# First stage of a two-layer pooling-and-attention block: pooling bands built on the chip, x loaded first, a new written order, and 32 transposes ahead of it

## The chip, the cores and the metric

The kernel runs on one core of a Trainium2 chip. The metric is device time in microseconds (us) from start to end of one execution. Before the change three runs took 1154.93, 1154.96 and 1155.19 us; the median is 1154.96 us. The core's engines each work through a queue of their own, in order: TensorE (PE in the profile, its weight loads PEld), VectorE (DVE), ScalarE (ACT), GpSimd (POOL) and SyncE (SP), which here issues the DMA transfers.

## The reference

The program computes two layers over 512 latent tokens and 256 context tokens of width 1024, in float32. Layer 0 mixes tokens by centred mean pooling, layer 1 by attention; each is followed by a squared-ReLU MLP with 4096 hidden units. The part that the change touches is the beginning of layer 0:

```python
def rms_norm(x, g):
    y = x * lax.rsqrt(jnp.mean(x * x, axis=-1, keepdims=True) + EPS)
    return y * g
...
m = (jax.nn.silu(cond) @ w + b)              # adaLN: shift, scale, gate for both halves of a layer
h_lat = modulate(rms_norm(x, g_mix_pre[i]), sh1, sc1)
y_lat = pool_mixer(h_lat, w_pool[j], pool_scale[j])
x = x + gt1 * rms_norm(y_lat, g_mix_post[i])
m_lat = sq_relu_mlp(modulate(rms_norm(x, g_mlp_pre[i]), sh2, sc2), w_mlp_in[i], w_mlp_out[i])
...
# pool_mixer: group g (256 channels) has window w = 2, 4, 8, 16
diff = mean over [t - w/2, t + w/2) of hf, minus hf
outs.append(diff @ w_pool[g])
```

The context tokens go through the same with their own conditioning vector. In layer 0 each of six modulation vectors (SH1, SC1, GT1, SH2, SC2, GT2) is a product of silu(cond) with a 1024 x 1024 block of `w_ada`.

## The kernel before

Tokens lie on the 128 partitions in six tiles t: 0 to 3 are latent, 4 and 5 context. `xr` holds the residual stream and `acc` what is being worked on. Products that need float32 accuracy are split in a high and a low part (hi and lo), and three products are summed.

The **first stage** is everything up to the first MLP group. Its steps stand in a table of words, `FIRST`, which is walked in order; while it is walked, the instructions of TensorE, VectorE and ScalarE are kept in the order in which they are recorded (`Kept`, lines 78 to 89). GpSimd and SyncE are not bound by it. The words, with the tile or channel block after the colon (a star puts a step on ScalarE rather than VectorE):

- `xs` sums the squares of a tile of x (ScalarE), `xe` adds epsilon (VectorE), `xp` takes the power -1/2 (GpSimd), `xn` scales the tile by it into `acc`.
- `edge` copies the inner band matrix and puts in the columns for the two ends of a sequence; `psm` and `psc` multiply a tile with its band on TensorE, which gives pooled mean minus identity, transposed (latent into `psm`, context into `psc`); `ev`, `evc` copy those results out of PSUM.
- `mm` is a conditioning product: one or two loads of 1 MB from `w_ada` (named `raw` in SBUF), multiplied on TensorE into `psada`; `rows`, `sel` and `mods` turn the result into columns. `SC1_0` to `SH1_3` come in eight loads, `GT1` in four, `SC2` and `SH2` in eight, twenty in all.
- `hi`, `lo` scale the pooled columns, `pool` multiplies them by `w_pool` (into `pspool`). Then, per tile: `ms` sums squares of the result, `rs` makes the reciprocal root, `c` copies, `b` multiplies by the gate, `r` adds to the residual, `s` and `rs2` are the next norm, `n` scales.
- `turn` transposes (into `psx`), `h` modulates, `xhi` and `xlo` split, `whi` and `wlo` split the first MLP weights, and `in` multiplies with them (into `psin`): this is the first group of the MLP, and the last thing in the table.

`rs` and `rs2` call a helper, `rstd`, that issues two GpSimd instructions, a TENSOR_SCALAR that adds epsilon (`ms` in the profile, lines 208 and 214) and the power (`rs`, line 216).

The inner bands (four windows, 128 x 144 each) and the edge columns come ready from the host in one transfer, `gate<-in_band`, of 128 x 640 numbers. SyncE issues the transfers in the order of the code: a small one with the conditioning vectors (`phase`), tiles 0 and 1 of x, the bands, tiles 2 to 5, `vec`, the pooling weights, then the `w_ada` loads. The buffers for `raw` come from two pools of four and three, by a list `turns`.

After the table, the first MLP goes on group by group on TensorE (lines 637, 761, 884), with VectorE and ScalarE preparing the weights and, for the following layers, the remaining modulation vectors on VectorE.

An activation function table is loaded into ScalarE when a function is not in the one that is loaded. To have the table of Exp at hand for the attention, `extra0` issues one Exp on a constant in group 2 of the first MLP (line 1108); the instruction depends on nothing else, and in the program it stands first in ScalarE's queue.

Of the kernel before, what the change touches and what calls it, by code (L numbers as in the profile page):

```python
# [17 lines left out]
P = 128  # L18
D = 1024
KT = D // P  # L20
# [21 lines left out]
xs:0 xe:0 xp:0 xn:0 xs:1 xe:1 xs:2 edge:0 xp:1 psm:0:2 xn:1 xs:3 psm:0:0 xe:2 psm:0:4 xp:2 psm:1:2 xs:4 xn:2  # L42
psm:1:4 psm:0:6 xe:3 xp:3 edge:1* psm:2:4 xe:4 psm:2:2 xp:4 xn:3 xs:5 psm:1:0 psm:3:4 psm:3:2 ev:4* xe:5 psm:2:0
xp:5 xn:4* psm:3:0 pw:0 ev:5* psm:1:6 wsc:0 psm:2:6 psm:3:6 pw:1 ev:7* ev:6 wph:0 wsc:1 mm:SC1_0 ev:0* psc:4:0
rows:SC1_0 xn:5 mm:SH1_0 wph:1 sel:SC1_0 ev:2* rows:SH1_0 psc:5:0 mods:SC1_0 psc:4:2 evc:0 sel:SH1_0 psc:5:2
mods:SH1_0 mm:SC1_1 wpl:0 hi:0 psc:4:6 rows:SC1_1 evc:2* psc:5:6 lo:0 hi:1 mm:SH1_1 sel:SC1_1 evc:6* psc:4:4
mods:SC1_1 psc:5:4 rows:SH1_1 lo:1 sel:SH1_1 evc:4* mm:SC1_2 mods:SH1_1 pool:0:0 rows:SC1_2 hi:2 wpl:1 pool:5:0
hi:3 sel:SC1_2 mm:SH1_2 lo:2 pool:1:0 mods:SC1_2 rows:SH1_2 sel:SH1_2 mm:SC1_3 mods:SH1_2 lo:3 hi:4 pool:4:0
pool:1:1 lo:4 mm:SH1_3 ms:1:0 rows:SC1_3 hi:5 pool:4:1 rows:SH1_3 c:1:0 sel:SC1_3 sel:SH1_3 pool:5:1 mods:SH1_3
mods:SC1_3 pool:0:1 lo:5 hi:7 mm:GT1_0a hi:6 lo:7 pool:0:2 mm:GT1_0b ms:4:0 lo:6 pool:5:2 rows:GT1_0 pool:0:3  # L50
c:4:0 sel:GT1_0 ms:0 mm:GT1_2a mods:GT1_0 gc:1:0 gc:0:0 psg:0:0 rs:0 c:0 pool:1:2 gate:0:0 mm:GT1_2b w_in
psg:1:0 rows:GT1_2 pool:1:3 gate:1:0 b:1:0 sel:GT1_2 pool:2:0 whi:0 mods:GT1_2 gc:0:1 gc:1:1 b:4:0 psg:0:1
ms:1:1 pool:5:3 wlo:0 gate:0:1 pool:4:2 rs:1 c:1:1* b:0 pool:4:3 ms:5 psg:1:1 b:1:1 pool:2:1 ms:4:1 rs:5 r:0
mm:SC2_0a c:4:1* gate:1:1 rs:4 mm:SC2_0b r:1 c:5* pool:2:2 s:0 b:4:1 pool:3:0 r:4 s:1 pool:3:1 rs2:0 pool:3:2
rows:SC2_0 s:4 rs2:1 pool:2:3 b:5 n:0* mm:SH2_0a rs2:4 n:1 mm:SH2_0b ms:2 r:5 sel:SC2_0 n:4* turn:0:1 rows:SH2_0
# [37 lines left out]

@with_exitstack
def backbone(ctx: ExitStack, tc, x, ctx_in, w_ada, w_pool, w_qkv, g_q, g_k, w_o, w_mlp_in,
             w_mlp_out, vecs, rope, band, out):
    nc = tc.nc
    ordered, mixed = [False], [False]
    sy, gp = nc.sync, nc.gpsimd
# [1506 lines left out]
```

## Time and profile before

| what | value |
|---|---|
| median of three runs | 1154.96 us |
| the profiled execution's own time | 1155.58 us |
| its span from first to last instruction | 1153.7 us |
| TensorE busy | 1135.3 us (98%) |
| VectorE busy | 930.9 us (81%) |
| ScalarE busy | 632.1 us (55%) |
| GpSimd busy | 71.1 us (6%) |
| TensorE's first matmul starts | 8.29 us |
| first matmul after the table (line 637) starts | 92.39 us |
| granted TensorE clock | 0.999 |

In a line of the timeline the first number is the start in us from the beginning of the span, the second the duration; then come engine, line, operation, output and input, the number of instructions taken together, and in brackets how long the engine had been idle and what released it. Nearly every instruction of the first stage has line 91, that of the helper that records it, so tiles and names tell the steps apart. The granted clock is a figure of the throttle; the rate at which TensorE takes its instructions is read from the starts of the matmuls.

### The profile page before, as it was taken

To read this page: it belongs to the slowest core of one execution; us is meant where nothing else is said; L and a number is where in the kernel's file an instruction comes from. 1 tells how busy PE (TensorE), PEld (TensorE's weight loads), DVE (VectorE), ACT (ScalarE), POOL (GpSimd) and SP (SyncE) were. 2 spreads that over 40 slices of the span, in tenths; PEclk is the share of its full clock that TensorE was granted. 3 is DMA by queue.
4 is the path that set the end of the run, shared out by engine and by line. 5 is a ranking of instruction groups with operands and counts; after the bars stand their busy time and mean duration, and the time that the engine had idled before them with its cause. 6 is when DMAs were issued, how large, how long until landed. Compare 5 with 4: busy or idle time off the path is not lost.

```text
span 1153.7 us, 16000 instructions
## 1 busy us (share of the span) xinstructions
PE 1135.3 (98%) x6200; PEld 988.7 (86%) x6200; DVE 930.9 (81%) x1517; ACT 632.1 (55%) x1082; POOL 71.1 (6%) x113
## 2 busy tenths in 40 slices
PE   7999999999999999999999999999999999999997
PEld 6779899988899988998887889988988888888886
DVE  4788588998988997996778699867787679778876
ACT  7687445554455444455675367753776435534523
POOL 1230000000000000000241200002100000000001
PEclk9999999999999999999999999999999999999999
DMA  9982233333343444333422102115243214313312
GB/s 376 419 350 75 74 116 113 137 120 141 113 150 140 146 147 146 120 137 115 177 74 73 37 1 74 38 74 186 106 159 133 91 56 146 110 45 138 110 33 114
DMA packets 25516, 147.34 MB, mean 128 GB/s; under 512 B 2784, under 2 KB 5344, under 8 KB 9696
## 3 DMA queue, kind: packets, MB, share of 16 engines
q1 hardware_dynamic: 25440, 146.32, 35.0%
q8 instruction: 49, 0.80, 0.3%
q14 instruction: 27, 0.22, 0.1%
HBM read 138.96 MB, written 7.34 MB: 127 GB/s over the span
## 4 chain that ended last, share of the span: by engine, by line
PE 90%; issue 3%; POOL 3%; DVE 2%; ACT 2%; DMA 0%; POOLq 0%; DVEq 0%; SPq 0%; ACTq 0%
PE pso L884 24%; PE psin L761 18%; PE psin L637 16%; PE pso L995 12%; PE psy L1421 3%; PE po L1396 3%; PE pss L1355 3%; PE psq L1141 2%; PE pspt L1377 2%; PE psin L91 2%; PE psada L91 1%; POOL rs L216 1%; PE psm L91 1%; PE pspool L91 1%; POOL rs L1150 1%
## 5 line engine op out<-in xcount | busy, mean ns | idle before, releaser
L884 PE MATMUL pso<-units,rb 128*128 128x512 f32 x1152 | 279.2, 392 | 0.0
L884 PEld LDWEIGHTS pso<-units,rb 128*128 128x128 f32 x1152 | 214.7, 188 | 41.0
L303 DVE SCALAR_TENSOR_TENSOR rows<-raw,cond,rows 128x256 f32<-128x256 f32 x280 | 127.0, 478 | 2.0
L898 DVE TENSOR_TENSOR acc<-acc,pso 128x512 f32<-128x512 f32 x126 | 83.9, 679 | 39.5 <-PE pso L884 39.4
L637 PE MATMUL psin<-ra,rb 128*128 128x512 f32 (+1 forms) x310 | 87.8, 360 | 0.0
L995 PE MATMUL pso<-units,pairs 128*128 128x512 f32 x336 | 82.7, 389 | 0.0
L637 PE MATMUL psin<-ra 128*128 128x512 f32 (+1 forms) x256 | 76.5, 376 | 0.0
L995 PEld LDWEIGHTS pso<-units,pairs 128*128 128x128 f32 x336 | 63.1, 188 | 13.1
L999 DVE TENSOR_TENSOR acc<-acc,pso 128x512 f32<-128x512 f32 x72 | 48.7, 682 | 26.3 <-PE pso L995 26.3
L214 POOL TENSOR_SCALAR ms<-ss 128x1 f32<-128x1 f32 x15 | 10.0, 666 | 938.2 <-ACT junk L201 917.0
L761 PE MATMUL psin<-ra,units 128*128 128x384 f32 x336 | 65.8, 337 | 0.4 <-ACT psin L773 0.4
L761 PE MATMUL psin<-sums,units 128*128 128x384 f32 x336 | 64.1, 337 | 0.0
L761 PEld LDWEIGHTS psin<-ra,units 128*128 128x128 f32 x336 | 59.9, 188 | 4.0 <-ACT psin L773 0.5
L637 PEld LDWEIGHTS psin<-ra,rb 128*128 128x128 f32 x310 | 55.6, 189 | 8.7
L761 PEld LDWEIGHTS psin<-sums,units 128*128 128x128 f32 x336 | 59.0, 188 | 1.6
L173 DVE TENSOR_TENSOR units<-raw,units 128x1024 fp32r<-128x1024 f32 (+2 forms) x49 | 55.1, 1150 | 6.3 <-ACT units L170 6.1
L170 ACT CAST units<-raw 128x1024 fp32r<-128x1024 f32 (+2 forms) x49 | 47.0, 995 | 17.6 <-PE pso L884 13.4
L637 PE MATMUL psin<-rb 128*128 128x512 f32 (+1 forms) x155 | 55.9, 362 | 0.6 <-DVE rb L1490 0.6
L637 PEld LDWEIGHTS psin<-ra 128*128 128x128 f32 x256 | 47.1, 188 | 8.7
L896 ACT COPY acc<-pso 128x512 f32<-128x512 f32 x48 | 27.1, 586 | 47.3 <-PE pso L884 46.6
L1141 PE MATMUL psq<-units,ra 128*128 128x512 f32 x216 | 52.2, 393 | 0.0
L637 PE MATMUL psin<-rb,ra 128*128 128x512 f32 (+1 forms) x128 | 48.1, 376 | 0.0
(291 smaller groups left out, 2386.5 us busy)
## 6 DMA issues: line engine op xcount, KB each, us to landing
raw<-in_w_ada SPq DMA_DIRECT2D x48, 1024.0 KB, 6.2
raw<-in_w_mlp_in SPq DMA_DIRECT2D x32, 1024.0 KB, 4.9
raw<-in_w_mlp_out SPq DMA_DIRECT2D x32, 1024.0 KB, 5.3
raw<-in_w_qkv SPq DMA_DIRECT2D x6, 1024.0 KB, 4.9
spill<-xr SPq DMA_DIRECT2D x10, 512.0 KB, 3.8
xr<-spill SPq DMA_DIRECT2D x10, 512.0 KB, 6.5
raw<-in_w_o SPq DMA_DIRECT2D x4, 1024.0 KB, 4.9
xr<-in_x SPq DMA_DIRECT2D x4, 512.0 KB, 5.2
```

Of the source, the lines that this page charges most:

```text
L91: return lambda *args, **kw: self.tc.keep_in_program_order(f(*args, **kw))
L170: a = sc.copy(hi, raw)
L173: b = ve.tensor_tensor(out=lo, in0=raw, in1=hi, op=ALU.subtract)
L303: ve.scalar_tensor_tensor(out=r, in0=raw[:, k, :], scalar=cond[:, k, c:c + 1], in1=r, op0=ALU.mult, op1=ALU.add)
L637: te.matmul(ps[:, bank, o:o + ln], w[:, k, fs], rhs, start=start, stop=(k == KT - 1 and n == 2), skip_group_check=len(ks) < KT or self.paired)
L761: te.matmul(bank, w[k], a[k], start=start and k == 0 and m == 0, stop=stop and k == 3 and m == 2, skip_group_check=True)
L884: te.matmul(pss[h][:, 0:cols[h][1]], a[:, f, ts_], w[:, f, cols[h][0]:sum(cols[h])], start=(n == 0 and not seeded[t]), stop=(n == len(seq) ...
L898: ve.tensor_tensor(out=d, in0=d, in1=ps[:, 0:w], op=ALU.add)
L995: te.matmul(ps, a, w, start=(m == 0), stop=(m == len(seq) - 1))
L999: ve.tensor_tensor(out=M[n][:, t], in0=M[n][:, t], in1=ps, op=ALU.add)
L1141: te.matmul(ps, a[:, k, sl], w[:, k % 4, :], start=(k == 0 and n == 0), stop=(k == KT - 1 and n == 2))
L1355: te.matmul(ps[:, c2, 0:384], a[:, sl], b[:, kv, 384 * c2:384 * c2 + 384], start=(n == 0), stop=(n == 2))
```

## The change

There are seven parts.

1. `FIRST` is a different order of the same steps, with `xn:0` in two halves, some steps moved between VectorE and ScalarE, and new steps `silu`, `re` and `re2`; `turns`, which assigns the `w_ada` loads to the two pools, is different too.
2. The inner bands are made on the chip: for each window GpSimd fills a 128 x 144 matrix with 1/w and cuts both sides off with two AFFINE_SELECT instructions; VectorE subtracts the identity from all four. Only the edge columns (128 x 64) are loaded.
3. Tile 0 of x is loaded first, then the edges, tiles 1 to 3, `phase`, the context tiles.
4. Epsilon in the norms of the stage is added on VectorE (`row_eps`, steps `re`, `re2`), and GpSimd keeps only the power.
5. Silu's table is loaded by an activation on a constant at the very start; the true Silu is a step of the table.
6. The Exp that fetches the attention's table is issued in group 4 of the first MLP and reads `grow`, which is loaded there.
7. TensorE opens with 32 transposes of the identity into a PSUM tile that nothing reads.

The order of the transfers on SyncE behind those of part 3 (pooling weights, the `w_ada` loads, the MLP weights) stays as it is.

```diff
 FIRST = """
-xs:0 xe:0 xp:0 xn:0 xs:1 xe:1 xs:2 edge:0 xp:1 psm:0:2 xn:1 xs:3 psm:0:0 xe:2 psm:0:4 xp:2 psm:1:2 xs:4 xn:2
...
+xs:0 xs:1 xe:0 edge:1 xp:0 edge:0 xs:2 xn:0:1 xn:0:0 xe:1 psm:0:2 xs:3 xe:2 xp:1 psm:0:4 xp:2 xn:1 psm:0:0 silu
...
 """
...
-    sy.dma_start(phase[:, 16:40], vecs[:, 160:184])
...
     xload(0)
-    xload(1)
-    sy.dma_start(gate.rearrange("p a n -> p (a n)")[:, 8 * BW:12 * BW + 64], band)
-    for t in range(2, NT):
+    sy.dma_start(gflat[:, 12 * BW:12 * BW + 64], edge)
+    for t in range(1, NL):
+        xload(t)
+    sy.dma_start(phase[:, 16:40], vecs[:, 160:184])
+    for t in range(NL, NT):
         xload(t)
     sy.dma_start(vec, vecs[:, 0:160])
-    sc.activation(cond[:, :, 0:2].rearrange("p k c -> p c k"), given.rearrange("p (c k) -> p c k", k=KT),
-                  AF.Silu)
+    for g in range(4):
+        w, rows = 2 << g, bands[:, 2, g, :]
+        gp.memset(rows, 1.0 / w)
+        gp.affine_select(out=rows, in_=rows, compare_op=ALU.is_ge, fill=0.0, base=HALO + w // 2,
+                         pattern=[[-1, BW]], channel_multiplier=1)
+        gp.affine_select(out=rows, in_=rows, compare_op=ALU.is_ge, fill=0.0, base=w // 2 - 1 - HALO,
+                         pattern=[[1, BW]], channel_multiplier=-1)
+    inner = bands[:, 2, :, HALO:HALO + P]
+    ve.tensor_tensor(out=inner, in0=inner, in1=ident.unsqueeze(1).broadcast_to([P, 4, P]), op=ALU.subtract)
+    sc.activation(sm_tile("sm")[:, 6:7], nhalf[:, 0:1], AF.Silu)
+
+    def silu():
+        sc.activation(cond[:, :, 0:2].rearrange("p k c -> p c k"), given.rearrange("p (c k) -> p c k", k=KT),
+                      AF.Silu)
...
-    def row_eps(t):
+    def row_eps(t, parts=1):
         ms = sm_tile("ms")
-        ve.tensor_scalar(out=ms[:, 0:1], in0=rs[t][:, 0:1], scalar1=EPS, scalar2=None, op0=ALU.add)
+        if parts == 1:
+            ve.tensor_scalar(out=ms[:, 0:1], in0=rs[t][:, 0:1], scalar1=EPS, scalar2=None, op0=ALU.add)
+        else:
+            ve.tensor_scalar(out=ms[:, 0:1], in0=rs[t][:, 1:2], scalar1=rs[t][:, 0:1], scalar2=EPS, op0=ALU.add,
+                             op1=ALU.add)
         rs[t] = ms
...
-    def row_scaled(t, on_act):
+    def row_scaled(t, on_act, h=None):
+        to, row = (z[:, t, :] if h is None else z[:, t, 512 * h:512 * h + 512] for z in (accv, xr))
...
+    def awake(n):
+        ps = psB.tile([P, 512], F32, tag="b", name="idle")
+        for k in range(n):
+            te.transpose(ps[:, (k % 4) * P:(k % 4 + 1) * P], ident, ident)
+
-    turns.extend((0, 0, 0, 0, 1, 1, 0, 0, 0, 0, 1, 1, 0, 0, 0, 0, 1, 1, 0, 0))
+    turns.extend((0, 0, 0, 0, 1, 1, 0, 0, 0, 0, 0, 0, 1, 1, 0, 0, 0, 0, 1, 1))
...
+    st.at(0.05, awake, 32)
...
-        ms=pool_ms, rs=lambda t: keep(rs, t, rstd, rs[t], 2 if t in (4, 1) else 1),
+        ms=pool_ms, re=lambda t: row_eps(t, 2 if t in (4, 1) else 1), rs=row_pow,
...
-        rs2=lambda t: keep(rs, t, rstd, rs[t], 1), n=lambda t, act: norm_c(t, act),
+        re2=row_eps, rs2=row_pow, n=lambda t, act: norm_c(t, act),
...
         if g == 4:
             head_gains()
+            sc.activation(sm_tile("sm")[:, 7:8], grow[:, 0, 0:1], AF.Exp, scale=0.0)
         if g > 1:
             ada_step()
-        if g == 2:
-            sc.activation(sm_tile("sm")[:, 7:8], nhalf[:, 0:1], AF.Exp)
```

How the built program's queues stand, at three places (a row is line, operation, output and input names, shape, and a count of like instructions in a row; one float32 instruction on TensorE stands as two records in the profile).

TensorE at its opening, before: the band products (`psm`) come first, then the transposes that spread the pooling scale (`psg`).

```order
L91 MATMUL psm<-gate,acc 128x136 x6
L91 MATMUL psm<-gate,acc 128x144 x4
L91 MATMUL psm<-gate,acc 128x136 x2
L91 MATMUL psm<-gate,acc 128x144 x6
L91 MATMUL psm<-gate,acc 128x136 x4
L91 MATMUL psm<-gate,acc 128x144 x2
L91 MATMUL psm<-gate,acc 128x136 x2
L91 MATMUL psg<-ident,phase 128x128 x4
```

TensorE at its opening, now:

```order
L92 MATMUL idle<-ident 128x128 x32
L92 MATMUL psm<-gate,acc 128x136 x8
L92 MATMUL psm<-gate,acc 128x144 x14
L92 MATMUL psm<-gate,acc 128x136 x2
L92 MATMUL psm<-gate,acc 128x144 x2
L92 MATMUL psm<-gate,acc 128x136 x6
L92 MATMUL psg<-ident,phase 128x128 x8
```

The 32 instructions of `psm` are the same in number; the 32 `idle` transposes stand ahead of them, and no `psg` stands between.

TensorE around the conditioning product SH1_3, the eighth of the twenty, before: the rows from SC1_2 (the first row) to SH1_3 (the last); `pspool` with x6 is one `pool` step, and x4 with `rows,sel` is a `sel`.

```order
L91 MATMUL psada<-raw,cond 32x256 x8
L91 MATMUL pspool<-rb,ra 128x256 x12
L91 MATMUL psada<-rows,sel 32x2x2 x4
L91 MATMUL psada<-raw,cond 32x256 x8
L91 MATMUL pspool<-rb,ra 128x256 x6
L91 MATMUL psada<-rows,sel 32x2x2 x4
L91 MATMUL psada<-raw,cond 32x256 x8
L91 MATMUL pspool<-rb,ra 128x256 x12
L91 MATMUL psada<-raw,cond 32x256 x8
```

The same stretch of TensorE now, again from SC1_2 to SH1_3:

```order
L92 MATMUL psada<-raw,cond 32x256 x8
L92 MATMUL pspool<-rb,ra 128x256 x6
L92 MATMUL psada<-raw,cond 32x256 x8
L92 MATMUL psada<-rows,sel 32x2x2 x4
L92 MATMUL pspool<-rb,ra 128x256 x6
L92 MATMUL psada<-rows,sel 32x2x2 x4
L92 MATMUL pspool<-rb,ra 128x256 x6
L92 MATMUL psada<-raw,cond 32x256 x8
L92 MATMUL pspool<-rb,ra 128x256 x6
L92 MATMUL psada<-rows,sel 32x2x2 x4
L92 MATMUL psada<-raw,cond 32x256 x8
```

Four `pool` steps stand ahead of SH1_3 where five stood, and three `sel` steps where two stood in this stretch.

ScalarE in the middle of the stage, before: from the first `s` (a square sum of `xr`) to the first two `h` steps (`acc<-psx`, two instructions each).

```order
L91 ACTIVATE junk,ss<-xr 128x1024 x3
L91 ACTIVATE acc<-xr,rs 128x1024
L91 ACTIVATE junk,ss<-pspool 128x1024
L91 ACTIVATE acc<-xr,rs 128x1024
L91 ACTIVATE junk,ss<-xr 128x1024
L91 ACTIVATE acc<-psx,mods_91,avec_94 128x2x128 x4
```

ScalarE at the same place now, from the first `s` to the second `h`:

```order
L92 ACTIVATE junk,ss<-xr 128x1024
L92 ACTIVATE junk,ss<-pspool 128x1024
L92 ACTIVATE junk,ss<-xr 128x1024
L92 ACTIVATE acc<-xr,rs 128x1024
L92 ACTIVATE junk,ss<-xr 128x1024
L92 ACTIVATE acc<-xr,rs 128x1024
L92 ACTIVATE junk,ss<-xr 128x1024
L92 ACTIVATE junk,ss<-pspool 128x1024
L92 ACTIVATE acc<-psx,mods_91,avec_94 128x2x128 x2
L92 CAST ra<-acc 128x4x128
L92 ACTIVATE acc<-xr,rs 128x1024
L92 ACTIVATE acc<-psx,mods_91,avec_94 128x2x128 x2
```

Eight instructions stand ahead of the first `h` where seven stood, two of them `n` steps (`acc<-xr`) as before and one more square sum of `pspool`; a third `n` step, that of tile 4, now stands behind the first `h` and its split.

82 lines of the change are left out of this document (38 added, 44 removed).

## The prediction

> **What bounds the kernel now.** I read the page's shares first, then the windows of the first 90 us, the timeline there, and the transfers' landings.
>
> ```profile
> PE 1135.3 (98%) x6200; PEld 988.7 (86%) x6200; DVE 930.9 (81%) x1517; ACT 632.1 (55%) x1082; POOL 71.1 (6%) x113
> PE 90%; issue 3%; POOL 3%; DVE 2%; ACT 2%; DMA 0%; POOLq 0%; DVEq 0%; SPq 0%; ACTq 0%
> ...
> 0.00:8.30 8.30, 0.01 (x1) 0.01 (x1) 2.29 (x9) 5.29 (x8) 1.81 (x8) 1.00 0.74 264
> 30.00:40.00 10.00, 10.00 (x132) 7.61 (x136) 8.51 (x22) 6.57 (x12) 0.00 (x0) 1.00 1.01 416
> 60.00:70.00 10.00, 8.29 (x119) 4.58 (x111) 7.56 (x16) 8.34 (x16) 4.71 (x7) 1.00 1.01 418
> 70.00:82.00 12.00, 12.00 (x124) 11.13 (x122) 10.69 (x18) 11.62 (x23) 4.35 (x7) 1.00 0.73 273
> ```
>
> TensorE carries 90% of the chain that ends last. In a window row the columns behind the length are PE, PEld, DVE, ACT, POOL, the clock, the DMA share and GB/s. TensorE does nothing for 8.3 us, then is full except between 60 and 70. But the DMA share is 1.01 as well (30:40 and 60:70): the twenty conditioning loads arrive as fast as the chip carries them. So two things bound this stage side by side, TensorE's work and the arrival of the loads, and the change touches both. What comes after 92 us is TensorE without a gap; what the stage gains or loses, I let through to the end at full value.
>
> **The opening.**
>
> ```profile
> 1.00 0.29 POOL masks.py:199 TENSOR_SCALAR_AFFINE_SELECT ident<-ident 128x128 f32<-128x128 f32 x1
> 1.15 0.89 SPq L234 DMA_DIRECT2D xr<-in_x  x2
> 4.83 1.06 ACT L91 ACTIVATE junk<-xr 128x1024 bf16<-128x1024 f32 x1 [0.73 <-DMA xr<-in_x]
> 6.25 0.56 POOL L492 TENSOR_TENSOR rs<-ms,nhalf 128x1 f32<-128x1 f32 x1 [4.96 <-DVE ms L91]
> 6.84 0.75 DVE L91 TENSOR_SCALAR acc<-xr,rs 128x1024 f32<-128x1024 f32 x1 [0.68 <-POOL rs L492]
> 7.57 0.66 DVE L91 COPY gate<-gate 128x576 f32<-128x576 f32 x2
> 8.29 9.27 PE L91 MATMUL psm<-gate,acc 128*128 128x136 f32 x52 [8.29 <-DVE gate L91]
> 17.83 1.61 PE L91 MATMUL psm<-gate,acc 128*128 128x144 f32 x12
> ...
> L91 PE MATMUL psm<-gate,acc 128*128 128x136 f32 x6 | 1.6, 434 | 0.0
> L91 PE MATMUL psm<-gate,acc 128*128 128x136 f32 x11 | 1.6, 279 | 0.0
> ```
>
> The first tile of x was issued second; issued first, at 0.72 where `phase` stood, it lands 0.4 us earlier, near 4.4, and its square sum is ready near 5.6. Meanwhile GpSimd makes the bands: four fills at some 0.2 and eight selects at 0.33 (0.29 scaled from 128 to 144 columns) on top of the identity end near 4.8, and VectorE's subtraction of 512 columns, estimated at 0.7 from the 0.66 copy, near 5.5. Then VectorE does both edge copies (2 x 0.66, one of them formerly on ScalarE) and the two halves of `xn:0` (0.75): first `psm` at 7.9 instead of 8.29. GpSimd's power (0.56) and the epsilon hide behind the edge copies.
>
> The last two rows are the same instruction early (8.9 to 10) and late (15 to 17.3): 434 against 279 ns, with the granted clock 1.00 in both. From the starts: 52 records from 8.29 to 17.40, where `psg` follows, take 0.175 each, the 12 from 17.83 on 0.121. At 0.121 the 52 would take 6.3 instead of 9.1 us, so the slow start costs 2.8. The 32 transposes start when the identity is there, near 1.9 since three fills stand ahead of its select, and at 0.22 for the first and 0.12 for the last end near 8; between 7 and 8.4 they cost nothing, as the bands' chain ends at 7.9 itself. If the rate rises during them, the 64 records of `psm` end at 7.9 + 7.7 = 15.6, and TensorE is 3.2 us ahead (0.4 + 2.8). If transposes of a constant do not raise it, 0.4. I take 3.2, since the rows show nothing but TensorE's own work going before the faster rate.
>
> [...]
>
> **The loads take most of it back.**
>
> ```profile
> gate<-in_band SPq DMA_DIRECT2D x1, 320.0 KB, 4.8
> 22.60 0.33 SPq L151 DMA_DIRECT2D raw<-in_w_ada  x1
> raw<-in_w_ada SPq DMA_DIRECT2D x1, 1024.0 KB, 13.4
> 36.13 1.07 PE L91 MATMUL psada<-raw,cond 128*32 128x256 f32 x16
> 38.35 1.63 PE pspool L91 x12
> 92.39 16.81 PE L637 MATMUL psin<-ra,units 128*128 128x384 f32 x96
> ```
>
> The load for SH1_3 is issued at 22.60 and lands 13.4 later, at 36.0; TensorE uses it at 36.13, so it has nothing in hand there. The bands' transfer shrinks from 320 to 32 KB. 1 MB takes 1024 KB / 416 GB/s = 2.5 us, so 288 KB are 0.7 us, and x begins 0.4 earlier; against that stand the edges' small rows. I take the loads 0.9 earlier (0.7 to 1.1): SH1_3 lands at 35.1. TensorE, 3.2 us ahead and with one `pool` step less to do before it, would be there near 32, so it waits some 3 us in all at the loads up to this one, and starts it 1.0 earlier. Behind SH1_3, TensorE before had 92.39 - 36.13 = 56.3 us to the end of the table, waits in it; now the moved `pool` step is to be done in addition, 0.8 (1.63 for two), less a `sel` of 0.1 drawn ahead: +0.7 or 0.8. So if nothing else changed the stage would end 0.2 earlier.
>
> **The waits at 60 us.** What can be won in addition is what TensorE waited there.
>
> ```profile
> 50.68 2.10 POOL L214 TENSOR_SCALAR ms<-ss 128x1 f32<-128x1 f32 x1 [4.01 <-ACT junk L91]
> 54.66 2.06 POOL L216 TENSOR_TENSOR rs<-ms,nhalf 128x1 f32<-128x1 f32 x1
> 60.97 0.57 POOL L216 TENSOR_TENSOR rs<-ms,nhalf 128x1 f32<-128x1 f32 x1
> 62.49 1.46 POOL L216 TENSOR_TENSOR rs<-ms,nhalf 128x1 f32<-128x1 f32 x1
> 61.41 0.33 PE L91 MATMUL psx<-ident,acc 128*128 128x128 f32 x1
> 62.38 0.55 PE L91 MATMUL psx<-ident,acc 128*128 128x128 f32 x3 [0.65 <-DVE acc L91]
> 64.20 0.25 PE L91 MATMUL psada<-work,sel 128*32 128x8 f32 x8 [0.27 <-DVE mods L91]
> 67.13 0.33 PE L91 MATMUL psx<-ident,acc 128*128 128x128 f32 x1 [0.27 <-ACT acc L91]
> 67.97 0.98 PE L91 MATMUL psx<-ident,acc 128*128 128x128 f32 x7 [0.52 <-DVE acc L91]
> ```
>
> The four gaps sum to 1.7 us as the profile models ends; by starts (a lone transpose takes 0.11) they are 2.2. I take 2.0. GpSimd was the cause: from the first of these rows to the last it runs 12 instructions back to back, 50.7 to 63.9, two per norm. With epsilon on VectorE half of them go, and GpSimd has room. VectorE gets an instruction of 0.15 each, which waits in its queue for ScalarE's sum: behind the one of tile 0's second norm stand a 0.7 us transpose of SC2_0 and the residual of tile 5.
>
> What is late next is ScalarE.
>
> ```profile
> 59.16 1.06 ACT L91 ACTIVATE junk<-xr 128x1024 bf16<-128x1024 f32 x1 [1.47 <-DVE xr L91]
> 60.22 1.14 ACT L91 ACTIVATE acc<-xr,rs 128x1024 f32<-128x1024 f32 x1
> 63.98 1.15 ACT L91 ACTIVATE acc<-xr,rs 128x1024 f32<-128x1024 f32 x1 [1.63 <-POOL rs L216]
> 66.08 1.91 ACT L91 ACTIVATE acc<-psx,mods,avec 128x256 f32<-128x256 f32 x4
> 68.02 0.62 ACT L91 CAST ra<-acc 128x512 fp32r<-128x512 f32 x1
> ```
>
> By TensorE's blocks (a `pool` 0.8, an `mm` 1.0, a `sel` 0.2, four transposes 0.45), it ends `pool:4:3` 18 us after SH1_3's start, at 53.1; ScalarE's square sum, two copies and gate behind that take 3, so its first `s` starts near 56. The eight instructions ahead of the first `h` take 1.06 to 1.2 each, 9.2, then come `h` (0.95), a split (0.55) and `n:4` (1.1): 67.9. TensorE wants `n:4` for `turn:4:0` 14.3 us after `pool:4:3`, at 67.4. That is a new wait of 0.5 (0 to 2.0, the old waits' size), and I take 0.6 with its followers. Of the old 2.0 then 1.4 is gained.
>
> [...]
>
> **Costed at nothing.** The Exp's table:
>
> ```profile
> 659.47 1.28 ACT L1360 ACT_TABLE_LOAD   x1
> 664.93 0.90 ACT L1360 ACTIVATE gate<-pss,sm 128x768 f32<-128x768 f32 x1 [4.17 <-DVE sm L1359]
> 213.44 0.49 ACT L783 ACTIVATE work<-psin 128x384 f32<-128x384 f32 x1 [0.96 <-PE psin L761]
> 218.78 0.46 ACT L769 COPY psin<-psin 128x384 f32<-128x384 f32 x1 [1.17 <-PE psin L761]
> ```
>
> Before, it was loaded at 659.47 with 4.17 us of idle time behind it, so removing that gains nothing. Now it stands ahead of the `work<-psin` at 213.44: 1.28 + 0.2 in a gap of 0.96, 0.5 late, made up by the next gap of 1.17. Without those gaps it would cost 1.5. The table load of the opening lies before x lands. `turns` changes which buffer a load takes; with four to five loads under way a buffer freed 2 us later still leaves the transfers full.
>
> **Sum.** Opening -3.2; waits for the loads +3.0; old waits -2.0; new +0.6: -1.6 us. The table ends at 90.8. The profiled execution, 1155.58 with a span of 1153.7, would be 1154.0; the median is 0.62 below it, which gives 1153.4. 0.2% is 2.3 us, about what a measurement of this kernel can tell from no change.
>
> **Rivals.** (a) *No new wait, and the loads 1.1 earlier*: -2.0 - 0.2 - 0.2 and up to 0.8 more if the searched order also closes small gaps: 1152.5 to 1151.8. For it: GpSimd is halved. Against: ScalarE's 11.62 of 12 us in 70:82. 0.27. (b) *ScalarE becomes the bound*: two more `n` (1.1 each) and one more copy (1.2) less an `h` (0.95) come to it, 2.4; it had 1.47 + 1.63 us of gaps at 59 and 64. Where those gaps cannot be used, the stage ends up to 2.4 later than before: 1155.0 to 1157.4. It costs the whole gain once ScalarE's first `h` comes at 67 instead of 65.3, and passes 0.2% slower at 69.2. 0.15, of which 0.08 beyond 0.2%. (c) *The bands come late* and the kernel is slower: GpSimd's selects take not 0.33 but 1.3 us (its powers reach 2.06), the bands end at 12.4, `psm` starts 7.4 later and, after an idle TensorE as at 8.29, costs the 2.8 again; 3 us of load waits cover some: +7.2, 1160.6. It passes 0.2% slower at 0.85 us a select. Against it is the 0.29 row. 0.04. (d) *The transposes do not raise the rate*: -0.4 in place of -3.2, but the load waits shrink with it from 3.0 to 0.2, since SH1_3 cannot start before its load: 1153.4 again. 0.04.
>
> **How the numbers follow.** The forecast has 0.50, from 1152.8 (no new wait) to 1154.8 (the old waits' size). Faster 0.27 from (a); slower 0.12 from (c) and half of (b); same 0.61 from the rest. The range takes in (a) and most of (b): 1151.6 to 1156.8.
>
> **What would show it.** `psm` near 7.9, its records at 279 ns from the start; TensorE idle or late at the loads between 18 and 35, SH1_3 near 35.1; no GpSimd TENSOR_SCALAR in the stage; `turn:4:0` near 68; the first matmul behind the table at 90.8. I am wrong if SH1_3 starts before 34.5, if the gaps after 60 sum to more than 2, or if the gain at the table's end is not there at the span's end.

## The result: 0.25% slower

Over 19 executions each, the kernel before took 1155.37 us (median; 1154.90 to 1156.22) and the changed kernel 1158.19 us (1156.26 to 1161.44). The ratio is 1.0025, with a 95% interval of 1.0018 to 1.0032. The prediction was 1153.4, within 1151.6 to 1156.8. Two things are to be explained: that the time is 2.8 us more where 2 us less were forecast, and that the executions of the changed kernel spread over 5.2 us where those of the kernel before spread over 1.3.

The profiled execution took 1157.12 us with a span of 1155.4; the one before had 1155.58 and 1153.7. First the page of the changed kernel (busy times, and the chain by engine), then the windows that answer those of the prediction and two more. The columns are as there.

```profile
PE 1140.6 (99%) x6232; PEld 992.5 (86%) x6232; DVE 932.1 (81%) x1532; ACT 633.1 (55%) x1081; POOL 65.1 (6%) x113
PE 90%; issue 2%; DVE 2%; ACT 2%; DMA 2%; POOL 1%; SPq 0%; POOLq 0%; DVEq 0%; ACTq 0%
```

```profile
0.00:8.30 8.30, 6.45 (x36) 6.34 (x37) 3.57 (x13) 3.78 (x6) 4.74 (x20) 1.00 0.75 254
18.00:21.00 3.00, 1.07 (x21) 0.44 (x22) 1.88 (x3) 1.94 (x3) 0.00 (x0) 1.00 1.00 412
60.00:70.00 10.00, 10.00 (x136) 6.89 (x136) 8.71 (x20) 9.78 (x17) 1.97 (x3) 1.00 1.00 413
85.00:90.00 5.00, 3.53 (x28) 3.12 (x26) 4.17 (x6) 4.83 (x8) 0.00 (x0) 1.00 0.24 102
```

The chain now has DMA at 2% (0% before) and POOL at 1% (3% before). The hole between 60 and 70 us is closed: TensorE 10.00 instead of 8.29. Two new holes stand at 18 to 21 (1.07 of 3) and at 85 to 90 (3.53 of 5). The timeline of TensorE shows the first of them; the first row is the start of the conditioning in the kernel before, the others are the changed kernel:

```profile
19.81 1.07 PE L91 MATMUL psada<-raw,cond 128*32 128x256 f32 x16
...
1.85 6.07 PE L92 MATMUL idle<-ident 128*128 128x128 f32 x32 [1.85 <-POOL ident masks.py:199]
7.79 2.12 PE L92 MATMUL psm<-gate,acc 128*128 128x136 f32 x16
10.65 6.04 PE L92 MATMUL psm<-gate,acc 128*128 128x144 f32 x48 [0.74 <-DVE acc L92]
17.96 1.07 PE L92 MATMUL psada<-raw,cond 128*32 128x256 f32 x16
20.96 1.07 PE L92 MATMUL psada<-raw,cond 128*32 128x256 f32 x16 [1.93 <-DMA raw<-in_w_ada]
36.12 1.07 PE L92 MATMUL psada<-raw,cond 128*32 128x256 f32 x16
```

The opening came as forecast: `psm` starts at 7.79 and its first 16 records take 2.12 us, the fast rate at once. The conditioning starts at 17.96 instead of 19.81. Then TensorE waits for the second load, and SH1_3 starts at 36.12, which is where it stood before (36.13). The second hole, at the end of the table, is in no step of the prediction. Here are, in turn, TensorE, ScalarE and VectorE of the changed kernel at the end of the table:

```profile
85.03 3.12 PE L92 MATMUL psin<-ra,rb 128*128 128x256 f32 x24
88.78 0.38 PE L92 MATMUL psin<-ra,rb 128*128 128x256 f32 x1 [0.64 <-ACT ra L92]
90.32 3.74 PE L92 MATMUL psin<-ra,rb 128*128 128x256 f32 x29 [1.16 <-DVE ra L92]
93.90 6.26 PE L656 MATMUL psin<-ra,units 128*128 128x384 f32 x35
```

```profile
85.31 1.02 ACT L92 ACTIVATE acc<-psx,mods,avec 128x256 f32<-128x256 f32 x2 [0.17 <-PE psx L92]
86.22 1.99 ACT L171 CAST units<-raw 128x1024 fp32r<-128x1024 f32 x2
88.11 1.14 ACT L92 CAST ra<-acc 128x512 fp32r<-128x512 f32 x2
```

```profile
87.30 2.36 DVE L174 TENSOR_TENSOR units<-raw,units 128x1024 fp32r<-128x1024 f32 x2 [0.83 <-ACT units L171]
89.58 1.29 DVE L92 TENSOR_TENSOR ra<-acc,ra 128x512 fp32r<-128x512 f32 x2
```

The last modulated block (`h`) is ready at 86.3. Its splits, `xhi` on ScalarE and `xlo` on VectorE, come at 88.11 and 89.58, since the casts of the next MLP weights (`units`) stand ahead of them on both engines. TensorE does 24 of its last 54 records, waits, does one, waits, and does the last 29. Before, the same casts stood behind the last split, and the 54 records ran through:

```profile
87.17 0.62 ACT L91 CAST ra<-acc 128x512 fp32r<-128x512 f32 x1
87.70 2.00 ACT L170 CAST units<-raw 128x1024 fp32r<-128x1024 f32 x2
```

```profile
85.83 6.71 PE L91 MATMUL psin<-ra,rb 128*128 128x256 f32 x54
```

These casts are not in the table. They split the first output weights of MLP 0, are recorded after it, and nothing keeps their place (`split` is called there without `pin`), so the scheduler put them there. The first matmul behind the table comes at 93.90 instead of 92.39, and from there both spans have the same length left: 1155.4 - 93.90 = 1061.5 and 1153.7 - 92.39 = 1061.3 us.

The longest times go with a lower clock. The mean granted clock of an execution is 0.994 to 0.996 in the four executions above 1160 us and 0.997 to 1.000 in the other fifteen; it does not order those fifteen (1157.85 us came with 1.000).

### The profile page after: what moved, and what is told of

It is laid out like the page before. It is cut to its first block, busy times and chain, and to the rows that moved or that the text cites. A ratio compares the mean times of both kernels' runs of the same rounds, so it can differ in the third digit from the quotient of the medians.

```text
span 1155.4 us, 16075 instructions
## 1 busy us (share of the span) xinstructions
PE 1140.6 (99%) x6232; PEld 992.5 (86%) x6232; DVE 932.1 (81%) x1532; ACT 633.1 (55%) x1081; POOL 65.1 (6%) x113
## 4 chain that ended last, share of the span: by engine, by line
PE 90%; issue 2%; DVE 2%; ACT 2%; DMA 2%; POOL 1%; SPq 0%; POOLq 0%; DVEq 0%; ACTq 0%
PE pso L909 24%; PE psin L780 18%; PE psin L656 16%; PE pso L1020 12%; PE psy L1445 3%; PE po L1420 3%; PE pss L1379 3%; PE psq L1165 2%; PE psada L92 2%; PE pspt L1401 2%; PE pspool L92 2%; PE psin L92 1%; DMA raw<-in_w_ada 1%; PE psx L92 1%; DMA xr<-in_x 1%
```

## The experiments

Times differ by some tenths of a us from one set of runs to the next, so each kernel is compared with runs of the kernel before taken beside it. Their median was 1155.69 us for the first four kernels told here, 1155.74 for epsilon on VectorE alone, the bands built in the kernel before and the Exp table, and 1155.18 for the rest.

**The casts.** One word keeps them behind the last split. (Some VectorE and TensorE instructions behind the table change places with it.)

```diff
-        wo_ = w_out(0, 0, one(unit[2]))
+        wo_ = w_out(0, 0, one(unit[2]), True)
```

> The changed kernel, with the casts of the first output weights of MLP 0 (units, two on ScalarE and two on VectorE) held behind the last splits of the opening table; nothing ahead of them is moved. Theory of the casts: in the changed kernel ScalarE's 1.99 us and VectorE's 2.36 us of casts stand ahead of the last splits and TensorE runs out of work between 85 and 90 us; with them behind, its last 54 psin records take about 6.7 us from 85.0 as before, the first matmul behind the table starts at 91.7 to 92.0 instead of 93.90, and the span is 1153.2 to 1153.6 instead of 1155.4. Theory of the chain: the last turned blocks themselves come late and the casts only fill a pause; then the first matmul behind the table stays within 0.4 us of 93.90 and the span within 0.4 of 1155.4. On the scatter (the changed kernel's times spread over 5 us, those of the kernel before over 1.3): if the pause of TensorE at 88 us starts it, the spread falls to under 2 us and the median by another 1 us; if not, only 2 us are gained and the spread stays.

Measured: 1154.95 us (1153.81 to 1157.55, 10 executions), ratio 0.9996 (0.9987 to 1.0005). The timeline of TensorE:

```profile
85.75 6.72 PE L92 MATMUL psin<-ra,rb 128*128 128x256 f32 x54
92.31 3.98 PE L656 MATMUL psin<-ra,units 128*128 128x384 f32 x22
```

The hole at the table's end is gone, so the theory of the casts holds. The first matmul behind the table is 0.3 us later than that theory gave; but from SH1_3's start to the first matmul behind the table it takes 92.31 - 36.88 = 55.4 us instead of 57.8 in the changed kernel. The spread, at 3.7 us, did not fall under 2. This execution's windows say why:

```profile
18.00:20.85 2.85, 0.74 (x16) 0.27 (x12) 1.48 (x2) 1.54 (x2) 0.00 (x0) 0.99 1.01 417
20.85:24.25 3.40, 3.40 (x37) 1.96 (x37) 0.54 (x2) 0.28 (x1) 0.00 (x0) 0.51 1.00 414
24.25:36.00 11.75, 11.75 (x155) 8.08 (x155) 9.26 (x26) 7.88 (x14) 0.00 (x0) 1.00 1.02 419
```

Behind the pause of 2.1 us at the second load, the granted clock is 0.51 in this window of 3.4 us, so about 1.7 us of work at the full clock are lost (an estimate, 0.49 of 3.4 us).

**The transposes.** Two kernels: the changed one without them, and the kernel before with them; no other instruction moves.

```diff
-    st.at(0.05, awake, 32)
+    st.at(0.05, awake, 0)
```

> The changed kernel without its 32 idle transposes; no other instruction moves. Theory that the loads hide the opening: the first 16 psm records take about 2 us longer and the conditioning starts near 19.5 instead of 17.96, but the wait for the second conditioning load (1.93 us before 20.96) shrinks by as much, and the first matmul behind the table stays within 0.4 us of 93.90. Rival, that the opening reaches the end: 1.5 to 2 us later. Rival on the scatter, that the early activity brings it (a lower granted clock later): the spread falls to under 2 us and the median by 1 us; if the transposes have no part in it the spread stays at 4 to 5 us.

Measured: 1157.85 us (1156.26 to 1158.90), ratio 1.0017 (1.0007 to 1.0026). The conditioning starts at 18.79 and the wait at the second load shrinks to 0.18; SH1_3 starts at 35.51. So the loads hide what the transposes win. The casts' hole is there, and in this execution the clock fell behind it:

```profile
85.00:90.10 5.10, 3.31 (x26) 2.90 (x25) 4.26 (x7) 5.10 (x8) 0.00 (x0) 1.00 0.12 51
90.10:93.50 3.40, 3.40 (x17) 3.40 (x18) 3.40 (x5) 1.55 (x3) 0.00 (x0) 0.50 0.87 301
```

That moved the first matmul behind the table to 95.02, where "within 0.4 us of 93.90" was expected. The spread of 2.6 us lies between what the two theories of the scatter gave (under 2, and 4 to 5).

```diff
-    st.at(0.5, pool_load)
+    st.at(0.05, lambda: [te.transpose(i[:, (k % 4) * P:(k % 4 + 1) * P], ident, ident) for i in (psB.tile([P, 512], F32, tag="b", name="idle"),) for k in range(32)]); st.at(0.5, pool_load)
```

> The kernel before with the 32 idle transposes alone; no other instruction moves. Theory that the loads hide the opening: the first 16 psm records go at the fast rate and the conditioning starts up to 2 us before 19.81, then TensorE waits about as long for the loads, and the first matmul behind the table stays within 0.4 us of 92.39; time within 0.5 us of the kernel before. Rival, that the opening is worth its length: 1.5 to 2 us less. Rival on the scatter, that the transposes bring it: the spread grows from 1.3 to 4 or 5 us and the median by 1 us.

Measured: 1155.83 us (1155.08 to 1157.27), ratio 1.0000 (0.9991 to 1.0010). The conditioning starts at 17.55 instead of 19.81, TensorE then waits 0.74, 1.10 and 0.34 us for three loads, and the first matmul behind the table stands at 92.86, 0.07 outside what was expected. The spread grew to 2.2 us, not to 4.

In neither kernel did the transposes bring SH1_3 forward: it starts 0.5 to 0.6 us later with them (36.12 against 35.51, and 36.60 against 36.13). In the changed order the second load itself lands later with them: at 20.83 us in the changed kernel, 20.61 with the casts behind and 20.31 with the pause filled (below), against 19.52 to 19.93 in the four versions here that build the bands and leave the transposes out. Most of these loads land 2.5 us after the one before; in the changed kernel this one takes 3.21, and in that stretch the view of the transfers has one packet of instructions (packets, MB, share of the time):

```profile
q8 instruction: 1, 0.02, 2.1%
```

With the transposes the first such packet after the start comes at 17.4 to 18.0 us in the changed order, without them at 23.2 to 24.3, and in each of the thirteen traces a load that lands behind this packet takes 2.8 to 4.0 us. So part of the wait for the second load seems to be of the transposes' own making; that the packet is the cause was not tested.

**The small transfer.** Is it a short-row transfer in mid-stream that held up x tile 2?

```diff
+    sy.dma_start(phase[:, 16:40], vecs[:, 160:184])
     xload(0)
...
-    sy.dma_start(phase[:, 16:40], vecs[:, 160:184])
```

> The changed kernel with the 12 KB transfer of phase (128 rows of 96 bytes) issued ahead of all x tiles, as the kernel before has it, instead of behind the four latent tiles. Theory of the short rows (an estimate from the two traces: 288 KB fewer were to be moved, and the load that ends the conditioning of SH1 still landed at 36.0 in both, with 319 GB/s from 5 to 8 us where it was 395): a transfer of 128 short rows costs the queue nearly as much as one of long rows once it runs full, and nothing while it starts up; then the landings from x tile 2 on come 0.3 to 0.6 us earlier than in the changed kernel (8.50, and 36.0 for that load). Rival, that only the time of issue counts: x tile 0 and all behind it land up to 0.4 us later. The time at the end by both: within 0.5 us of the changed kernel, since the pause at 88 us is not touched.

Measured: 1159.96 us (1159.44 to 1161.22, 4 executions), ratio 1.0037 (1.0023 to 1.0052). My theory of the short rows fell: tile 2 is used at 8.88 instead of 8.58, and the second load at 21.75 instead of 20.96. Later is what the rival gave, though tile 0, at 5.10 instead of 4.45, comes by more than its 0.4. The pause there grew to 2.42 us, and the clock was half for twice as long:

```profile
22.45:29.25 6.80, 6.80 (x55) 4.45 (x48) 3.63 (x9) 2.21 (x4) 0.00 (x0) 0.50 1.01 420
```

So "the time within 0.5 us of the changed kernel" failed too; in this execution the clock, which had not been counted, took 3.4 us of it (half of 6.8).

**Both edits together**: the casts behind, no transposes.

> The two edits together: casts of the output weights behind the last splits, and no idle transposes. Theory of the clock: the run with the casts behind (median 1154.95, spread 3.7 us) showed a granted clock of 0.50 from 21 to 24 us, behind TensorE's pause of 2.1 us at 18.6 to 20.7; without the transposes that pause was 0.18 us and the clock stayed at 1.00 there. So here the clock stays at 1.00 to the table's end, the first matmul behind the table starts at 91.3 to 91.8, the median is 1153.6 to 1154.5 and the spread under 2 us; 1.0 to 2.0 us below the kernel before. Rival, that the transposes do save time: 1155 or more, with the first matmul behind the table at 92.5 or later. Rival, that the scatter of the run with the casts behind comes from a later place: median as there, 1154.7 to 1155.2, spread 3 to 4 us.

Measured: 1154.24 us (1153.89 to 1154.77, 11 executions), ratio 0.9992 (0.9984 to 1.0001). Its TensorE:

```profile
7.74 9.61 PE L92 MATMUL psm<-gate,acc 128*128 128x136 f32 x64 [7.74 <-DVE ms L92]
18.62 1.07 PE L92 MATMUL psada<-raw,cond 128*32 128x256 f32 x16
20.07 1.07 PE L92 MATMUL psada<-raw,cond 128*32 128x256 f32 x16 [0.38 <-DMA raw<-in_w_ada]
35.94 1.07 PE L92 MATMUL psada<-raw,cond 128*32 128x256 f32 x16 [0.18 <-DMA raw<-in_w_ada]
84.85 6.72 PE L92 MATMUL psin<-ra,rb 128*128 128x256 f32 x54
91.40 4.85 PE L656 MATMUL psin<-ra,units 128*128 128x384 f32 x27
```

The theory of the clock held: 91.40 lies in the 91.3 to 91.8 that it gave, the clock is 1.00 to the table's end, and the spread is 0.9 us. The gain on the kernel before, 0.94 us, is just under the 1.0 that was expected, and the interval of the ratio still takes in 1.

**The pause filled.** The version with the casts behind and all 32 transposes, with 14 more of them in the pause:

```diff
-ev:2* mm:SC1_0 wsc:1 wph:0 mm:SH1_0 rows:SC1_0 psc:5:0 rows:SH1_0 sel:SC1_0 evc:0* sel:SH1_0 mods:SC1_0 psc:4:2
+ev:2* mm:SC1_0 wsc:1 wph:0 idle:14 mm:SH1_0 rows:SC1_0 psc:5:0 rows:SH1_0 sel:SC1_0 evc:0* sel:SH1_0 mods:SC1_0 psc:4:2
...
-        silu=silu, xs=row_square, xe=row_eps, xp=row_pow, xn=row_scaled, edge=band_edge, psm=band_mm, psc=band_mm, pw=pool_weights,
+        idle=awake, silu=silu, xs=row_square, xe=row_eps, xp=row_pow, xn=row_scaled, edge=band_edge, psm=band_mm, psc=band_mm, pw=pool_weights,
```

> The version with the casts behind and with the 32 idle transposes, and 14 idle transposes more between the first and the second conditioning load's matmuls, where TensorE paused for 2.1 us; by the 1.04 us of eight psg transposes they take 1.8 us, inside the pause. Theory of the clock: the pause is what lowers the granted clock to 0.50 in some executions; filled, the spread falls from 3.7 to under 2 us, the granted clock is 1.00 from 18 to 36 us, and the median falls by 0.5 to 1.2 us, to 1153.8 to 1154.5. Rival, that the clock falls for another reason (the early activity itself, or later pauses): median and spread as in the version with the casts behind, 1154.95 and 3 to 4 us.

Measured: 1154.79 us (1154.22 to 1155.56), ratio 0.9997 (0.9987 to 1.0006).

```profile
18.00:21.00 3.00, 3.00 (x38) 2.08 (x38) 1.79 (x3) 1.82 (x2) 0.00 (x0) 1.00 1.02 418
```

The spread fell from 3.7 to 1.3 us with no work taken away, which speaks for the pause and against the early activity. The expected gain in the median did not come: the ratios are 0.9996 without the filling and 0.9997 with it. The lowest time is higher, too (1154.22 against 1153.81, although the kernel before was 0.5 faster beside it), so the filling costs about what it saves; TensorE waits 1.17 us at another load and starts SH1_3 at 36.56. With the version that has both edits, four kernels now stand in a square (19, 10, 10 and 11 executions, row by row):

| | casts ahead | casts behind |
|---|---|---|
| 32 transposes (pause of 1.9 to 2.1 us at 19 to 21) | 1156.26 to 1161.44, spread 5.2 | 1153.81 to 1157.55, spread 3.7 |
| no transposes (pause of 0.2 to 0.4 us) | 1156.26 to 1158.90, spread 2.6 | 1153.89 to 1154.77, spread 0.9 |

Each pause adds spread, and with neither there is hardly any beyond that of the kernel before (0.9 against 0.7 us beside it). The version with both edits and the one with the pause filled come from a set of runs in which the kernel before spread over 0.7 us; beside the two versions with one edit it spread over 1.1, beside the changed kernel over 1.3.

**Epsilon.** Two kernels: the version with both edits with epsilon on GpSimd again, and the kernel before with epsilon on VectorE.

```diff
-re=lambda t: row_eps(t, 2 if t in (4, 1) else 1)
+re=lambda t: row_eps(t, 2 if t in (4, 1) else 1, gp)
...
-re2=row_eps
+re2=lambda t: row_eps(t, 1, gp)
```

> The version with both edits, and the epsilon of the norms of the pooled and the residual rows (not of the first x tiles) added on GpSimd again, as in the kernel before; the other engines' order is the same but for the eleven instructions that VectorE no longer has. Theory of the prediction (the old waits near 60 us were GpSimd's, and were worth 2.0 us): TensorE waits again for 1.5 to 2 us between 55 and 65 us, the first matmul behind the table comes 1.5 to 2 us later than in the version with both edits, and the time is 1.5 to 2 us more. Rival, that the new order of the table takes the waits away whatever engine adds epsilon: within 0.4 us of the version with both edits.

Measured: 1154.18 us (1153.86 to 1154.59), ratio 0.9992 (0.9983 to 1.0001): nothing changed. The order of the table closes the hole by itself; TensorE is full although GpSimd is as busy as in the kernel before (4.74 and 4.71 us):

```profile
60.00:70.00 10.00, 10.00 (x141) 6.67 (x143) 8.48 (x19) 9.78 (x16) 4.74 (x10) 1.00 1.01 416
```

```diff
-rs=lambda t: keep(rs, t, rstd, rs[t], 2 if t in (4, 1) else 1)
+rs=lambda t: keep(rs, t, rstd, rs[t], 2 if t in (4, 1) else 1, ve)
...
-rs2=lambda t: keep(rs, t, rstd, rs[t], 1)
+rs2=lambda t: keep(rs, t, rstd, rs[t], 1, ve)
...
-    def rstd(ss, parts):
+    def rstd(ss, parts, gp=gp):
...
-        gp.tensor_tensor(out=r[:, 0:1], in0=ms[:, 0:1], in1=nhalf[:, 0:1], op=ALU.pow)
+        nc.gpsimd.tensor_tensor(out=r[:, 0:1], in0=ms[:, 0:1], in1=nhalf[:, 0:1], op=ALU.pow)
```

> The kernel before with the epsilon of the pooled and the residual rows' norms added by VectorE and no longer by GpSimd; TensorE's, ScalarE's and SyncE's order is the same. Theory of the prediction (the waits of 1.71 us in the 60 to 70 us window were GpSimd's): those waits go, the first matmul behind the table comes 1.5 to 2 us before 92.39, and the time is 1.5 to 2 us less than the kernel before. Theory of the order, after the version with epsilon put back on GpSimd came out equal (1154.18 against 1154.24): the waits stay where they are, the table ends within 0.4 us of 92.39 and the time is within 0.4 us of the kernel before. Third: VectorE's queue, which now waits for each mean square, holds up what stands behind it, and the table ends 0.5 us or more later.

Measured: 1153.74 us (1153.40 to 1154.11), ratio 0.9983 (0.9973 to 0.9992): 2.0 us less than the kernel before. I had come to lean to the theory of the order; in the old order, the prediction's theory was the right one.

```profile
60.00:70.00 10.00, 9.82 (x133) 6.28 (x126) 9.14 (x22) 9.84 (x18) 3.41 (x5) 1.00 1.01 416
36.45 1.07 PE L91 MATMUL psada<-raw,cond 128*32 128x256 f32 x16
90.69 1.55 PE L637 MATMUL psin<-ra,units 128*128 128x384 f32 x8
```

From SH1_3 to the first matmul behind the table it takes 54.24 us where the kernel before took 92.39 - 36.13 = 56.26. This small part of the change, alone, has the lowest ratio here and beats both kernels.

**The bands.** Again from both sides: loaded again in the version with both edits, and built in the kernel before.

```diff
-    sy.dma_start(gflat[:, 12 * BW:12 * BW + 64], edge)
+    sy.dma_start(gflat[:, 8 * BW:12 * BW + 64], edge)
...
-    for g in range(4):
-        w, rows = 2 << g, bands[:, 2, g, :]
...
-    arrays["in_edge"] = _band_edges()
+    arrays["in_edge"] = _pool_bands()
```

> The version with both edits, with the bands loaded in the place of the edges' transfer (320 KB instead of 32 KB, as the kernel before had it) and not built by GpSimd. Theory of the bytes: 288 KB at 415 GB/s put each later landing off by 0.7 us, and with TensorE bound by the loads up to 36 us the table ends 0.5 to 0.7 us later. Rival, that the short transfer left the queue unfilled anyway (319 GB/s from 5 to 8 us in the changed kernel, 395 in the kernel before): landings from x tile 2 on within 0.2 us of the version with both edits, and the time within 0.3.

Measured: 1155.29 us (1154.91 to 1155.64), ratio 1.0001 (0.9992 to 1.0010), 1.05 us more than with the bands built. But the bytes are not the reason: x tile 2 is used at 8.04 instead of 8.43, and SH1_3 starts at 35.80 instead of 35.94. (That tile 2 came earlier means nothing by itself: in the seven versions of the changed order that load only the edges and issue `phase` where it does, it lands anywhere from 7.95 to 8.50 us, and here at 7.96.) What is longer is the way from there to the table's end, by 0.7 us, and it has one hole, at the transposes of tile 4. First ScalarE, then TensorE:

```profile
67.12 1.15 ACT L92 ACTIVATE acc<-xr,rs 128x1024 f32<-128x1024 f32 x1
68.18 1.00 ACT L92 ACTIVATE acc<-psx,mods,avec 128x256 f32<-128x256 f32 x2
```

```profile
69.23 0.66 PE L92 MATMUL psx<-ident,acc 128*128 128x128 f32 x4 [0.66 <-ACT acc L92]
```

TensorE starts when ScalarE has read the transposes of the tile before out of PSUM (68.18 + 1.00), almost 1 us after the scaled tile is ready (67.12 + 1.15). A PSUM buffer that is not yet free would look like this; why it shows only in this kernel, and the other 0.4 us of the 1.05, stay open.

```diff
-    sy.dma_start(gate.rearrange("p a n -> p (a n)")[:, 8 * BW:12 * BW + 64], band)
+    sy.dma_start(gflat[:, 12 * BW:12 * BW + 64], band)
...
+    for g in range(4):
+        w, rows = 2 << g, bands[:, 2, g, :]
...
-    arrays["in_band"] = _pool_bands()
+    arrays["in_band"] = _band_edges()
```

> The kernel before with the bands built by GpSimd and only the edges loaded, in the place of the band transfer; the rest of its order is the same. Theory of the bytes: as loading the bands again cost the version with both edits 1.05 us, building them takes 0.6 to 1.0 us off the kernel before, with landings from x tile 2 on 0.5 to 0.7 us earlier. Rival, that the kernel before is bound by TensorE from its first psm record (at 8.3 us) on and not by landings: the psm records start 0.5 us or more earlier, TensorE then waits for the loads, and the time stays within 0.4 us. What speaks for the rival: the kernel before shows no wait of TensorE for a load up to 42 us.

Measured: 1155.76 us (1155.43 to 1156.18), ratio 1.0001 (0.9992 to 1.0011). With 288 KB fewer to load, x tile 2 is used 0.2 us earlier (8.37 instead of 8.56), SH1_3 at 36.53 not earlier than the 36.13 of before, and the time is the same. The rival held in the time, and in part by its reason: `psm` starts at 8.41, no earlier than before, but the conditioning starts at 18.99 instead of 19.81, and TensorE then waits 0.59 us for a load.

**The Exp table**, in its old place:

```diff
-            sc.activation(sm_tile("sm")[:, 7:8], grow[:, 0, 0:1], AF.Exp, scale=0.0)
...
+        if g == 2: sc.activation(sm_tile("sm")[:, 7:8], nhalf[:, 0:1], AF.Exp)
```

> The version with both edits, with the Exp table warmed at the start as in the kernel before; ScalarE then has four table loads (Silu, Exp, Silu again and Exp in the attention) where that version has two; nothing else moves. Theory of the prediction (the move of the Exp load is worth nothing): within 0.4 us of the version with both edits (1154.24). Rival, that a load of 1.28 us in the attention stands on the path: 0.8 to 1.3 us more. The second Silu load, between the squares of the x tiles near 10 us, is covered by the loads by the first and adds another 1 us by the second.

Measured: 1154.42 us (1153.91 to 1154.61), ratio 0.9988 (0.9979 to 0.9997), against 0.9992 for the version with both edits. The table loads are worth nothing that can be seen in either place.

## Why the prediction was wrong, step by step

The term that failed most is the one that the prediction did not write down: the end of the table. Most of the terms can be read off the kernels without the casts' hole. Where TensorE stands at SH1_3's start and at the first matmul behind the table:

| kernel | SH1_3 starts | behind the table | between |
|---|---|---|---|
| predicted | 35.1 | 90.8 | 55.7 |
| before | 36.13 | 92.39 | 56.26 |
| changed | 36.12 | 93.90 | 57.78 |
| casts behind | 36.88 | 92.31 | 55.43 |
| casts behind, no transposes | 35.94 | 91.40 | 55.46 |
| before, epsilon on VectorE | 36.45 | 90.69 | 54.24 |

And the windows from 5 to 8 us, first of the kernel before, then of the changed one, on which the third point rests (the last number is GB/s):

```profile
5.00:8.00 3.00, 0.00 (x0) 0.00 (x0) 1.32 (x4) 2.12 (x4) 0.82 (x2) 1.00 1.03 395
5.00:8.00 3.00, 3.00 (x20) 2.89 (x19) 2.10 (x8) 1.74 (x4) 1.03 (x2) 1.00 0.92 319
```

- **Opening -3.2**: half right. `psm` started at 7.79 (7.9 forecast) and ran at the fast rate from its first record (16 in 2.12 us, 0.13 each, where the kernel before took 0.175). Its end came 0.9 us later than the 15.6 given (`psg` starts at 16.53), because VectorE's epsilon of x tile 2, which lands no earlier than before, stands ahead of the scaling of tile 1. The loads hide this.
- **Waits for the loads +3.0**: right as a mechanism. With and without the transposes SH1_3 starts at 36.12 and 35.51 in the changed kernel, and at 36.60 and 36.13 in the kernel before. In size it was 1.93 us, at one load.
- **Loads 0.9 us earlier**: wrong. SH1_3 started at 36.12 and not at 35.1. The step that failed took 288 KB at 416 GB/s off every later landing; x tile 0 did land 0.4 earlier, but tile 2 landed at 8.50 where it had landed at 8.47, and in no version of the changed order before 7.95, where 0.9 us would have made it 7.6; from 5 to 8 us the queue moved 319 GB/s where it had moved 395. The two kernels on the bands show that these bytes do not set the landings: in the changed order without the transposes SH1_3 starts at 35.80 with 320 KB loaded and at 35.51 to 35.94 with 32. What delays tile 2 is open.
- **Moved `pool` step +0.7 to 0.8**: too small for what the new order costs behind SH1_3. The version with both edits needs 55.46 - 54.24 = 1.2 us more there than the old order with epsilon on VectorE; what the rest of the 1.2 is, no run shows.
- **Old waits -2.0**: right to 0.02 us in size (56.26 - 54.24), and GpSimd was the cause in the old order. In the new order the waits would be gone in any case.
- **New wait +0.6 at the first transposes of tile 4**: did not come, as rival (a) had it. ScalarE had `n:4` ready at 68.62, 0.2 us ahead of TensorE's transposes at 68.85, where the forecast had it 0.5 behind.
- **The table's end**: missing from the prediction. The forecast took the way from SH1_3 to be 55.7 us; without the casts' hole it is 55.46, with it 57.78. The hole is worth 2.3 us. The step that failed is the one that carried the old 56.3 us behind SH1_3 over to the new order, changed only by the `pool` step and the waits near 60 and 67 us: a hole in the last 54 `psin` records was put at nothing without a reason. I had looked at the order inside the table and not at what the scheduler put between its last rows from behind it, where ScalarE has two casts ahead of the last two splits.
- **Carried to the end at full value**: right. Behind the table 1061.1 to 1061.6 us remain, in the changed kernel and in the experiments. TensorE is not without a gap there, but its gaps are the same: it is busy for 1052.9 of 1061.3 us in the kernel before and for 1053.1 of 1061.5 in the changed one.
- **From the profiled execution to the median**: 0.62 us were taken off, from three executions of the kernel before; over 19 its median was only 0.2 below the profiled one. And the changed kernel's median is 1.07 us above its profiled execution, in which the clock stayed at 1.00 at both pauses. A clock that falls in other executions would explain it: in three profiled executions of its variants one fall cost 1.7 us, or 3.4. That is my estimate; no trace shows a fall at these pauses in the changed kernel itself.

The sum of what was missed: loads 1.0, casts 2.3, the new order -0.2, median of the kernel before 0.4, and 1.3 (1.07 + 0.21) that the median of the changed kernel lies higher above its profiled execution than that of the kernel before, put down to the clock; together 4.8 us, and 1153.4 + 4.8 = 1158.2.

Of the rivals, (c) fell (GpSimd's selects end at 4.04). Rival (d) priced right what the transposes gain, nothing, but its premise that they do not raise the rate was wrong (the 16 `psm` records behind them took 2.12 us): that price was right by luck. Rival (b) gave 1155.0 to 1157.4 with ScalarE late; ScalarE was late, by two casts that it did not name and not by norms.

## What to carry to other kernels

When a written order is changed, look at its last rows together with the free work that is recorded behind it: an instruction that nothing holds goes into the first gap, and there it delays the step on which TensorE waits. Work that brings TensorE earlier to a load that has not landed gained nothing here (SH1_3 starts at 36.12 us with the transposes, at 35.51 without), and the longer pause can come with a lower clock: behind 2.1 us of pause it was 0.51 for 3.4 us with the casts behind, where the times spread over 3.7 us with the transposes and over 0.9 without. Try the parts of a change alone: here one of them was worth 2.0 us, and the whole lost 2.8.

## What the runs showed of the hardware that was not expected

Pauses of TensorE of 2.1 and 2.4 us, and one of 0.6 and 1.2 us with a single record between, were followed in profiled executions by a granted clock of 0.50, for 3.4, 6.8 and 3.4 us (casts behind, `phase` first, no transposes). In the changed kernel's own profiled execution pauses of 1.93 us and of 0.64 and 1.16 us, at the same two places, left it at 1.00. So pauses of about this length were followed by a lower clock in some of these executions and not in others. Kernels without such pauses spread over 0.7 to 1.3 us.

What decides is open. Here are the 3.4 us ahead of the falls, with the casts behind, without the transposes, and with `phase` first; TensorE's busy time is the number behind the length:

```profile
17.37:20.78 3.41, 1.30 (x23) 0.55 (x23) 2.11 (x3) 2.17 (x3) 0.00 (x0) 1.00 1.02 418
86.67:90.09 3.42, 1.63 (x12) 1.22 (x11) 3.15 (x4) 3.42 (x6) 0.00 (x0) 1.00 0.00 0
19.01:22.43 3.42, 1.00 (x21) 0.50 (x16) 1.17 (x2) 1.10 (x2) 0.00 (x0) 1.00 1.02 426
```

TensorE was busy for 1.00 to 1.63 us of them. But in the changed kernel it was busy for 1.48 and 1.62 us of the 3.41 us that end with its two pauses (at 20.96 and 90.32 us), and the clock of the next 3.41 us was 1.00. So the busy time just ahead does not tell by itself. No run shows why the clock stayed at 0.50 for twice as long in the version with `phase` first.

For the slow start the traces give no clock. The prediction read a granted clock of 1.00 beside the slow `psm` records, but the records of the clock begin only at 14.09 us in the kernel before, 5.8 us after its first matmul; ahead of the first record a window shows 1.00 all the same. TensorE has 25 records in the 5.8 us up to there (0.23 us each) and 18 in the 2 us from 14 to 16 (0.11 each). What sets the slower rate was not shown.

The 32 transposes of a constant were enough to give the next matmuls the fast rate: 16 `psm` records in 2.12 us, where without transposes 64 took 9.61. And a transfer made smaller by 288 KB, in the middle of a full queue, did not bring the landings behind it forward by its 0.7 us: x tile 2 was used 0.2 us earlier in the kernel before, and in the changed order its landing with the full transfer (7.96) lies within what it is without (7.95 to 8.50).
